# A two-layer decoder trunk in fp32: TensorE in the order of the program's text, and an order of the mixers made from stated latencies

## The chip, the core and the metric

The kernel runs on one core of a Trainium2 chip (trn2). Five engines work side by side, each through its own row of instructions: TensorE (PE, with its weight loads as PEld), VectorE (DVE), ScalarE (ACT), GpSimd (POOL) and SyncE (SP), which here only issues the DMAs that load weights. An engine starts its instructions in the order of its row, and a semaphore holds an instruction back until what it needs is done. The metric is device time in microseconds (us) of one execution, the median of several.

## What is computed

256 tokens of width 1024 go through two layers and a final norm. A layer is this (cut from the reference):

```python
def layer(x):                                   # x (1, 256, 1024), fp32
    x = x + 0.5 * swiglu_ffn(rms_norm(x), w_gate, w_up, w_down)     # ffn1, F = 2816
    h = rms_norm(x); z = h @ w_in               # one projection, columns split:
    y_a = mlstm_branch(...)                     # A: mLSTM matrix memory, 4 heads
    y_b = s5_branch(...)                        # B: S5 complex diagonal scan, then a GLU
    y_c = gla_branch(...)                       # C: gated linear attention, 4 heads
    y_d = rwkv7_branch(...)                     # D: RWKV-7 delta rule, 8 heads
    gates = sigmoid(gate_pre + gate_bias)       # 4 x 1024 columns of z
    merged = gates[0]*y_a + gates[1]*y_b + gates[2]*y_c + gates[3]*y_d
    x = x + merged @ w_out
    x = x + cross_attention(rms_norm(x), rms_norm(mem), wq, wk, wv, wo)  # 4 heads, 256 memory rows
    return x + 0.5 * swiglu_ffn(rms_norm(x), ...)                   # ffn2
```

All of it is in fp32. A product of fp32 accuracy is made of three products of rounded operands (`whi·xhi`, `whi·xlo`, `wlo·xhi`), so each block of weights costs three matmuls.

## The kernel before

**Tiling.** Activations stand transposed, as tiles of 128 channels by 256 tokens; `x` is eight of them. A matmul has a 128x128 block of weights and 256 columns. Weights come in chunks of 512 KB (`chunk`): SP loads one into one of three raw buffers `wraw`, ACT rounds it to `whi` (L243), DVE subtracts to get `wlo` (L244), both into one of four buffers, and TensorE multiplies. Half a megabyte of weights thus takes one ACT step and one DVE step and feeds 24 matmuls. A PSUM tile of 128x512 holds two products of 256 columns side by side.

**Stages of a layer.** `ffn1`: 22 products `gu` and the products `dn` back into `x` (L411). `mix`: the columns of `w_in` (`zin`), the four mixers and the gates. `mix_out`: four chunks of `wout` accumulated in four PSUM tiles `acc`; the last chunk adds each result to `x` (L579). `xattn`: queries `qps`, softmax, heads, and `wo` through the same `acc` code (`proj_k`). `ffn2` like `ffn1`. A norm needs the mean square of `x` for each token: eight squares (L292, L294), a matmul `ss` over the channels (L297), ten or eleven small DVE steps of a Newton iteration for the reciprocal root (L268 to L273), and a matmul `rp` that spreads the result over the partitions (L281).

**What sets the order.** Only SP's row is the order of the text (`manual_schedule` on SP alone). The rows of TensorE, DVE, ACT and POOL are made by a scheduler from dependencies, priorities and its own timeline; it may put a matmul of a later statement between two of an earlier one. In the mix the text itself is an interleaving: the mixers S (S5), G (GLA), M (mLSTM) and the dense work D (gates and the key and value products of the memory) are generators, and `ORDER` (L29 to L30) names for each layer which of them goes on next. RWKV (R) stands ahead of them all as one block. The four merges of the branches stand behind them.

**Places that the prediction steps through.** `gates` (L1522): for each of 16 chunks of a layer two products `gps` of 24 matmuls, side by side in one 128x512 tile, each followed by an ACT step `gst` (L1534). `proj_k` (L567): for `d` of 0 to 7 a product into half `d % 2` of tile `acc[d // 2]`, and in the last chunk the addition to `x` after each. In RWKV the small products with `thw` and `tha` (L1307 and on), the triangular solve `Tp` (L1417, L1419), the tiles `VU` and `Tw`. `mem_stats` (L444): the norm of the memory rows, called at `f == 10` of the first `ffn1`. `merge` (L1539): products `yps` and a DVE step `gld` (L1579).

Of the kernel before, what the change touches and what calls it, by code (L numbers as in the profile page):

```python
# [18 lines left out]
P = 128  # L19
# [6 lines left out]
MEM_AT = 0, 0  # L26
# [49 lines left out]
class K:  # L76
    def __init__(self, tc, ins, out, stages=None, layers=NL, taps=None):
        self.tc = tc
        self.nc = tc.nc
        self.ins = ins  # L80
        self.out = out
        self.layers = layers
        self.stages = stages
        self.taps = taps or {}
        self.uid = 0
        self.n_r, self.n_w, self.arena = 3, 4, 5248
        self.mem = self.kv = self.mcol = None
        self.loaded = False
        self.br, self.pdt = "n", ("psd", 2)
# [29 lines left out]
    def run(self):  # L119
        with ExitStack() as es:  # L120
# [12 lines left out]
            es.enter_context(self.tc.manual_schedule(engines={mybir.EngineType.SP}))  # L133
# [150 lines left out]
    def rstd_tok(self, x, last=False):  # L284

        nc = self.nc
        br, self.br = self.br, "n"
        ps = self.px([P, 512], "ss")
        acc = self.sp.tile([P, T], F32, tag="sa", name=self.nm("sa"), bufs=1)
        for k, xk in enumerate(self.tiles(x)):  # L290
            sq = acc if k == 0 else self.sp.tile([P, T], F32, tag="rA", name=self.nm("sq"), bufs=3)
            nc.scalar.activation(sq, xk, AF.Square)  # L292
            if 0 < k < (7 if last else 8):
                nc.gpsimd.tensor_tensor(acc, acc, sq, ALU.add)  # L294
        for tt in range(2):
            for i, s in enumerate((acc, sq) if last else (acc,)):
                nc.tensor.matmul(ps[:, 256 * tt:256 * tt + 1], s[:, tt * P:(tt + 1) * P], self.col[:, 0:1],  # L297
                                 start=(i == 0), stop=(i == int(last)))
# [6 lines left out]
    def rstd_row(self, x):  # L305

        rs = self.sp.tile([P, T], F32, tag="rs", name=self.nm("rs"), bufs=1)
        self.rows(self.rstd_tok(x), rs)
        return rs

# [18 lines left out]
    def norm(self, x, gname, rs=None):  # L329

        nc = self.nc
        rs = rs if rs is not None else self.rstd_row(x)
# [45 lines left out]
    def ffn(self, which):  # L378
# [6 lines left out]
        for f in range(22):  # L385
            blk = self.chunk(gu[l, f])
            ps = self.pd("gu")
            self.prod(blk, ps, hi, lo, f == 0)
            if f == 0:
                rs = self.rstd_row(self.x).unsqueeze(1).to_broadcast([P, 2, T])  # L390
# [7 lines left out]
            if f == 10 and self.mcol is None:  # L398
                self.mem_stats()
# [44 lines left out]
    def mem_stats(self):  # L444
# [3 lines left out]
        y = self.rstd_tok(self.mem_tiles())  # L448
        self.nc.vector.tensor_copy(self.mcol, y)
        self.rows(y, self.mrow)  # L450
# [7 lines left out]
    def mem_kv(self):  # L458
# [4 lines left out]
        for c in range(4):  # L463
            ps = self.pd("kps")
            self.prod(self.chunk(self.ins["wk"][l, c]), ps, mhi, mlo)
# [5 lines left out]
        for h in range(4):  # L471
            blk = self.chunk(self.ins["wv"][l, h])
            ps = self.pd("vps")
            for tt in range(2):
                for k in range(8):
# [13 lines left out]
    def xattn(self):  # L489
        nc, l = self.nc, self.l  # L490
        self.pdt = "psd", 2
        if self.kv is None:
            self.mem_gained()
            for _ in self.mem_kv():
                pass
# [11 lines left out]
        for c in range(2):  # L507
            q_of(c)
        y = self.rstd_tok(self.x)
# [3 lines left out]
        es = [self.softmax(0, qs, rq, kT)]  # L513
        q_of(2)
        es.append(self.softmax(1, qs, rq, kT))
        oh = [self.head(0, es[0], v)]
        q_of(3)
        for h in range(2, 4):
            es.append(self.softmax(h, qs, rq, kT))
            oh.append(self.head(h - 1, es[h - 1], v))  # L520
        self.proj_k("wo", 0, *oh[0], acc)
        oh.append(self.head(3, es[3], v))
        for h in range(1, 4):
            self.proj_k("wo", h, *oh[h], acc)
# [23 lines left out]
    def head(self, h, e, v):  # L548
# [7 lines left out]
        self.split(pt, *pT)  # L556
        ops = self.px([P, 2, T], "ops")
# [9 lines left out]
    def proj_k(self, wname, c, hi, lo, acc):  # L567
# [3 lines left out]
        for d in range(8):  # L571
# [31 lines left out]
    def wtiles(self, c):  # L603
        nc, l = self.nc, self.l
        self.mark(f"col{c}")
        blk = self.chunk(self.ins["win"][l, c])
        ps = self.pd("zin")
        if c < LAZY[self.l]:
            self.prod(blk, ps, *self.early, c == 0)
# [3 lines left out]
        self.prod(blk, ps, self.hi, self.lo)  # L613
        return ps

    def mix(self):
        nc, l = self.nc, self.l
        self.pdt = "psd", 2
        st = self.stages
        on = lambda s: st is None or "mix" in st or s in st  # L620
        self.early = self.gained(self.x, "mix_norm")
        with self.tc.high_priority():
            self.rs = self.rstd_row(self.x)
# [7 lines left out]
        with self.tc.issue_after(self.normed.ins):  # L631
            if on("mixd"):
                self.ys[3] = self.rwkv()
            live = {"S": on("mixb") and self.s5(), "G": on("mixc") and self.gla(), "M": on("mixa") and self.mlstm(),
                    "D": self.dense([b for b, n in ((2, "mixc"), (1, "mixb"), (0, "mixa"), (3, "mixd")) if on(n)])}
            branch = {"S": "s", "G": "g", "M": "g", "D": "d"}
            for c in ORDER[self.l]:
                if live[c]:
                    self.br = branch[c]
                    next(live[c], None)  # L640
            for c in "SGMD":
                self.br = branch[c]
                for _ in live[c] or ():
                    pass
        names = {2: "proj_c", 0: "proj_a", 1: "glu", 3: "proj_d"}
        for b in (2, 1, 0, 3):
            if b in self.ys:
                self.merge(b, self.ys[b], names[b])
# [4 lines left out]
    def dense(self, branches):  # L653

        for i, b in enumerate(branches):
# [1093 lines left out]
```

## Time and profile before

| | |
|---|---|
| runs | 1852.25, 1852.32, 1857.06 us; median 1852.32 |
| profiled execution | 1860.55 us, span of the profile 1858.8 us |
| busy over the span | PE 1794.1 us (97%), DVE 1302.3 (70%), ACT 912.2 (49%), POOL 527.5 (28%) |
| matmul instructions | 14884 in the trace |
| TensorE clock granted, mean | 0.979 |
| DMA | 320.35 MB, 172 GB/s mean |

A busy engine is not an engine at full rate: matmul records overlap, so the count of matmuls in a stretch says more than the busy time. The granted clock is the clock of TensorE as the profile records it; 1.00 is 2.4 GHz, and the lower of its two levels, 1.2 GHz, shows as 0.5 for the time that it lasts. The span lies 1.75 us under the execution's own time.

### The profile page before, as it was taken

How to read it: one execution, taken by the hardware profiler on the slowest of the kernel's cores; microseconds unless marked ns; L12 is line 12 of the kernel's file. 1: busy time of each engine (PE TensorE's matmuls, PEld its weight loads, DVE VectorE, ACT ScalarE, POOL GpSimd, SP SyncE). 2: the span in 40 equal slices, each digit the busy share in tenths (PEclk: the TensorE clock that was granted, in tenths of full speed). 3: DMA queues.
4: the chain of work that ended last, by engine and by line, in shares of the span. 5: the costliest groups of instructions: out<-in, count | busy, mean ns of one | idle time of the engine just before them, and what ended most of it. 6: DMA issues, size and time to landing. Idle time of an engine off the chain costs nothing.

```text
span 1858.8 us, 37108 instructions
## 1 busy us (share of the span) xinstructions
PE 1794.1 (97%) x14884; PEld 1757.8 (95%) x14884; DVE 1302.3 (70%) x2197; ACT 912.2 (49%) x1434; POOL 527.5 (28%) x733
## 2 busy tenths in 40 slices
PE   7989999989999999999999999999999999999997
PEld 7989998989999998999999999998989999999997
DVE  8876586896576776666597767696935667667653
ACT  4444455455554455444445445535544544545442
POOL 6699321150011210000154995103121103110001
PEclk9989999999999999999999999988989999999999
DMA  5656554537446654556556666644534676446653
GB/s 194 185 159 186 174 190 140 162 120 228 130 148 218 236 183 124 173 183 185 171 175 211 181 178 191 181 117 149 177 104 127 201 262 218 148 127 190 183 182 103
DMA packets 131853, 320.35 MB, mean 172 GB/s; under 512 B 45792, under 2 KB 50912, under 8 KB 131168
## 3 DMA queue, kind: packets, MB, share of 16 engines
q1 hardware_dynamic: 83664, 290.31, 50.2%
q10 hardware_dynamic: 48016, 27.67, 5.2%
q8 instruction: 116, 1.90, 0.4%
q14 instruction: 57, 0.47, 0.1%
HBM read 300.11 MB, written 16.52 MB: 170 GB/s over the span
## 4 chain that ended last, share of the span: by engine, by line
PE 51%; DVE 4%; issue 3%; DMA 2%; POOL 2%; ACT 1%; ACTq 0%; POOLq 0%; DVEq 0%
PE gu L259 6%; PE gu L258 6%; PE gu L260 6%; PE dn L258 3%; PE dn L259 3%; PE dn L260 3%; PE acc L576 2%; DVE wlo L244 1%; PE gps L259 1%; PE zin L258 1%; PE gps L258 1%; PE zin L260 1%; PE zin L259 1%; PE gps L260 1%; PE gu L354 1%
## 5 line engine op out<-in xcount | busy, mean ns | idle before, releaser
L244 DVE TENSOR_TENSOR wlo<-wraw,whi 128x1024 fp32r<-128x1024 f32 x524 | 673.7, 1287 | 352.3 <-ACT whi L243 345.3
L243 ACT CAST whi<-wraw 128x1024 fp32r<-128x1024 f32 x524 | 546.9, 1047 | 620.6 <-issue 154.7
L260 PE MATMUL gu<-xhi,wlo 128*128 128x256 f32 x1344 | 382.0, 284 | 2.9 <-DVE wlo L244 2.9
L258 PE MATMUL gu<-xhi,whi 128*128 128x256 f32 x1344 | 382.0, 284 | 0.0
L259 PE MATMUL gu<-xlo,whi 128*128 128x256 f32 x1344 | 381.7, 284 | 0.0
L260 PEld LDWEIGHTS gu<-xhi,wlo 128*128 128x128 f32 x1344 | 259.2, 193 | 3.5 <-DVE wlo L244 3.5
L258 PEld LDWEIGHTS gu<-xhi,whi 128*128 128x128 f32 x1344 | 259.1, 193 | 0.1
L259 PEld LDWEIGHTS gu<-xlo,whi 128*128 128x128 f32 x1344 | 259.1, 193 | 0.0
L294 POOL TENSOR_TENSOR arena<-arena 128x256 f32<-128x256 f32 x69 | 73.4, 1064 | 547.2 <-ACT arena L292 544.4
L260 PE MATMUL dn<-ahi,wlo 128*128 128x256 f32 x704 | 199.5, 284 | 1.0 <-DVE wlo L244 1.0
L258 PE MATMUL dn<-ahi,whi 128*128 128x256 f32 x704 | 199.2, 284 | 0.0
L259 PE MATMUL dn<-alo,whi 128*128 128x256 f32 x704 | 199.2, 283 | 0.0
L258 PE MATMUL gps<-hhi,whi 128*128 128x256 f32 x512 | 152.2, 298 | 4.5 <-ACT gst L1534 3.6
L259 PE MATMUL gps<-hlo,whi 128*128 128x256 f32 x512 | 150.2, 294 | 0.0
L260 PE MATMUL gps<-hhi,wlo 128*128 128x256 f32 x512 | 147.8, 290 | 0.0
L260 PEld LDWEIGHTS dn<-ahi,wlo 128*128 128x128 f32 x704 | 135.1, 192 | 1.4 <-DVE wlo L244 1.4
L259 PEld LDWEIGHTS dn<-alo,whi 128*128 128x128 f32 x704 | 135.1, 192 | 0.1
L258 PEld LDWEIGHTS dn<-ahi,whi 128*128 128x128 f32 x704 | 134.9, 192 | 0.3
L258 PE MATMUL zin<-hhi,whi 128*128 128x256 f32 x384 | 113.5, 296 | 4.1 <-ACT VU L1399 4.1
L260 PE MATMUL zin<-hhi,wlo 128*128 128x256 f32 x384 | 112.4, 293 | 0.0
L259 PE MATMUL zin<-hlo,whi 128*128 128x256 f32 x384 | 112.2, 292 | 0.0
L258 PEld LDWEIGHTS gps<-hhi,whi 128*128 128x128 f32 x512 | 101.0, 197 | 8.2 <-ACT gst L1534 5.0
(529 smaller groups left out, 4413.2 us busy)
## 6 DMA issues: line engine op xcount, KB each, us to landing
wraw<-in_gu_dram SPq DMA_DIRECT2D x176, 512.0 KB, 3.8
wraw<-in_dn_dram SPq DMA_DIRECT2D x88, 512.0 KB, 4.1
wraw<-in_win_dram SPq DMA_DIRECT2D x68, 512.0 KB, 4.1
wraw<-in_gates_dram SPq DMA_DIRECT2D x64, 512.0 KB, 4.1
gd<-gst ACTq DMA_DIRECT2D x32, 256.0 KB, 2.1
wraw<-in_wk_dram SPq DMA_DIRECT2D x16, 512.0 KB, 3.7
wraw<-in_wv_dram SPq DMA_DIRECT2D x16, 512.0 KB, 3.6
gld<-gd SPq DMA_DIRECT2D x32, 256.0 KB, 4.0
```

The costliest lines, as they stand in the source:

```text
L243: nc.scalar.copy(hi, raw)
L244: nc.vector.tensor_tensor(lo, raw, hi.bitcast(F32), ALU.subtract)
L258: nc.tensor.matmul(ps, w[0], x[0], start=first, stop=False)
L259: nc.tensor.matmul(ps, w[0], x[1], start=False, stop=False)
L260: nc.tensor.matmul(ps, w[1], x[0], start=False, stop=last)
L294: nc.gpsimd.tensor_tensor(acc, acc, sq, ALU.add)
L354: self.nc.tensor.matmul(ps[:, s, :], w[wi], x[xi], start=(k == 0 and s == 0 and i == 0), stop=(k == 7 and i == 2), skip_group_check=True)
L576: nc.tensor.matmul(ps, w[wi], x[:, k, :], start=(c == 0 and d % 2 == 0 and k == 0 and i == 0), stop=(c == 3 and k == 1 and i == 2), skip_g ...
```

## The change

TensorE joins SP in `manual_schedule`, so its row is the order of the text, and the text is written anew where that matters. In the mix, `ORDER` goes. `drive` goes through the generators R, S, G, M and, in the first layer, N (the memory's norm, moved here from `ffn1`). A generator yields a number: how long, in microseconds of TensorE work, the operands of its next piece will take. `pe_us` sums TensorE's work in the text so far at 0.12 us for a matmul of 256 columns, and `drive` takes the first generator whose time has come, else a piece of the dense work. `BEGIN` says when each generator starts. A yield of -1 asks for a turn at once, and after `SMALL` us of small work the dense work gets a turn.

```diff
-ORDER = ("SSDSSSDSSSGSDSSGSDSGDGDGDGDGDGDDGDGDGMDGMDGMMDMDMMDMDDDDDD",
-         "SSSSSSSSSSSSDSDGDGDGDMGDMGDMGDMGDMGDMGDMGDMGDGDGDDDDDDDDDD")
+BEGIN = {"R": 0, "S": 38, "G": 120, "M": 190, "N": 60}, {"R": 0, "S": 0, "G": 100, "M": 170, "N": 0}
+SMALL = 4.0
...
-            es.enter_context(self.tc.manual_schedule(engines={mybir.EngineType.SP}))
+            es.enter_context(self.tc.manual_schedule(engines={mybir.EngineType.SP, mybir.EngineType.PE}))
...
+    def drive(self):
+        t0 = self.pe_us()
+        gens = {"R": self.rwkv(), "S": self.s5(), "G": self.gla(), "M": self.mlstm()}
+        if self.mcol is None:
+            gens["N"] = self.mem_stats()
...
+        ready = {c: t0 + BEGIN[self.l][c] for c in gens}
+        dense, run = self.dense(gens), 0.0
+        while gens or dense:
+            t = self.pe_us()
+            can = [c for c in gens if ready[c] <= t]
+            if dense and (not can or run > SMALL and can[0] != "R"):
+                self.br, run = "d", 0.0
+                if next(dense, None) is None:
+                    dense = None
+                continue
+            c = can[0] if can else min(gens, key=ready.get)
+            self.br = branch[c]
+            lat = next(gens[c], None)
+            now = self.pe_us()
+            if lat is None:
+                del gens[c]
+            elif lat < 0:
+                ready[c], run = now, 0.0
+            else:
+                ready[c], run = now + lat, run + now - t
...
+    def pe_one(self, i):
...
+        return 0.12 * n / 256 if mov.dtype == F32R else 2 * 0.00084 * max(n, m, 32)
...
     def gates(self, br):
...
-            self.gated, self.gated2 = nc.scalar.dma_start(gd[dp], g), self.gated
-            yield
+                if s:
+                    self.gated, self.gated2 = nc.scalar.dma_start(gd[dp], g), self.gated
+                yield
...
-            if f == 10 and self.mcol is None:
-                self.mem_stats()
...
     def mem_stats(self):
...
+        sums = self.squares(self.mem_tiles())
+        yield 14
+        y = self.rstd_tok(sums)
         self.nc.vector.tensor_copy(self.mcol, y)
+        yield 6
         self.rows(y, self.mrow)
```

Besides: in an FFN the squares stand ahead of the products, `ss` stands behind product 1 and `rp` behind product 2, and the steps of the first three products on DVE and ACT are held back until then. In `xattn` the parts of the heads stand in another order. The merges of S and G move into the dense work, the gate columns 9, 10, 13 and 14 of `w_in` too, and all merges use the two PSUM buffers of the dense work where they had four of their own. In RWKV the tile `L` is split in two, with 16 DVE steps of half the size for each 8 and 4 more ACT DMAs in each layer, `VU` and `Kt` become separate tiles, the solve gets a high priority on DVE, and a yield of 45 stands ahead of the products with `Tw` that need it. The scratch arena shrinks from 5248 to 3776 columns. Both programs have the same 13946 matmul instructions.

What moved, at three places. First **TensorE in the gates** of layer 0, where a gate's chunk is multiplied; `gps` is the product's tile with its number, `hhi` and `hlo` the normed input. Before, the end of a half of tile 4734 and the start of the second half of tile 4660:

```order
L258 MATMUL gps_4734<-hhi_2775,whi 128x256
L259 MATMUL gps_4734<-hlo_2776,whi 128x256
L260 MATMUL gps_4734<-hhi_2775,wlo 128x256
L258 MATMUL gps_4660<-hhi_2775,whi 128x256 [waits Activation_49]
L259 MATMUL gps_4660<-hlo_2776,whi 128x256
L260 MATMUL gps_4660<-hhi_2775,wlo 128x256
```

Now, the end of the first half of tile 4927 and the start of its second half:

```order
L260 MATMUL gps_4927<-hhi_2842,whi 128x256
L261 MATMUL gps_4927<-hlo_2843,whi 128x256
L262 MATMUL gps_4927<-hhi_2842,wlo 128x256
L260 MATMUL gps_4927<-hhi_2842,whi 128x256 [waits Activation_49]
L261 MATMUL gps_4927<-hlo_2843,whi 128x256
L262 MATMUL gps_4927<-hhi_2842,wlo 128x256 [waits DVE_49]
```

Before, a half of another tile stood between the two halves of a tile; now the second half follows the first at once, and its first matmul waits for ACT, which reads the first half. This is so at 15 of the 32 chunks; at the others another branch's work stands between.

Second **TensorE at the end of `wout`** in layer 0, the last chunk, whose results DVE adds to `x`; `acc` with its number is the tile, `mghi` and `mglo` the merged input. Before, the even `d` of all four tiles (7305 to 7308) and then the odd ones; here the change from the one to the other:

```order
L576 MATMUL acc_7308<-mghi_7483,wlo 128x256
L576 MATMUL acc_7308<-mghi_7483,whi 128x256
L576 MATMUL acc_7308<-mglo_7484,whi 128x256
L576 MATMUL acc_7308<-mghi_7483,wlo 128x256
L576 MATMUL acc_7305<-mghi_7483,whi 128x256 [waits DVE_49]
L576 MATMUL acc_7305<-mglo_7484,whi 128x256
```

Now, tile 7328 with `d` = 0 and then `d` = 1:

```order
L624 MATMUL acc_7328<-mghi_7506,whi 128x256
L624 MATMUL acc_7328<-mglo_7507,whi 128x256
L624 MATMUL acc_7328<-mghi_7506,wlo 128x256
L624 MATMUL acc_7328<-mghi_7506,whi 128x256 [waits DVE_49]
L624 MATMUL acc_7328<-mglo_7507,whi 128x256
L624 MATMUL acc_7328<-mghi_7506,wlo 128x256
```

Before, 18 matmuls of three other tiles stood between the two halves of a tile; now the second half follows at once and waits for DVE's addition. The same holds for the other tiles and for `wo`: 16 places in two layers.

Third **the memory's norm**. TensorE before, in `ffn1`, where `ss` of the memory rows stands among the products `gu`:

```order
L259 MATMUL gu_1318<-xlo_138,whi 128x256
L260 MATMUL gu_1318<-xhi_137,wlo 128x256
L258 MATMUL gu_1318<-xhi_137,whi 128x256 [waits Activation_49]
L259 MATMUL gu_1318<-xlo_138,whi 128x256
L297 MATMUL ss_1081<-consts,arena 128x1 [waits PE_49,Pool_49]
L297 MATMUL ss_1081<-consts,arena 128x1
L260 MATMUL gu_1318<-xhi_137,wlo 128x256 [waits DVE_49]
L258 MATMUL gu_1318<-xhi_137,whi 128x256
```

TensorE now, in the mix of layer 0, at `rp` of the memory rows, 48 matmuls `gps` and 8 small ones behind `ss`:

```order
L260 MATMUL gps_3797<-hhi_2842,whi 128x256
L261 MATMUL gps_3797<-hlo_2843,whi 128x256
L262 MATMUL gps_3797<-hhi_2842,wlo 128x256
L283 MATMUL rp_3894<-consts,arena 128x128 [waits DVE_49,Activation_49]
L283 MATMUL rp_3894<-consts,arena 128x128
L1316 MATMUL yps_3898<-us_3440,s5In_1273 128x64 [waits PE_49]
L1316 MATMUL yps_3898<-us_3440,s5In_1273 128x64 x3
L260 MATMUL gps_3903<-hhi_2842,whi 128x256 [waits PE_49]
```

DVE before, in the same stretch of RWKV's work (`kk`, `KB`, `tha`) and S5's (`bb`, `ba`):

```order
L1239 SCALAR_TENSOR_TENSOR bb_4178<-consts,ba_4177 128x64 [waits DVE_49]
L1239 SCALAR_TENSOR_TENSOR bb_4178<-consts,ba_4177 128x64 x7
L244 TENSOR_TENSOR wlo<-wraw,whi 128x1024 [waits DMAHW2_49,PE_49,Activation_49]
L1351 SCALAR_TENSOR_TENSOR kk_3268<-tha_3237,kk_3268 128x1024 [waits DVE_49]
L1255 TENSOR_TENSOR arena<-arena,yps_4061 128x256 [waits DVE_49]
L1241 TENSOR_TENSOR ba_4177<-bb_4178,bC_469 128x512 [waits DVE_49]
L244 TENSOR_TENSOR wlo<-wraw,whi 128x1024 [waits DMAHW3_49,PE_49,Activation_49]
L1353 SCALAR_TENSOR_TENSOR KB_3310<-kk_3268,em_3266 128x8x64 [waits DMAHW4_49,DVE_49]
L1353 SCALAR_TENSOR_TENSOR KB_3310<-kk_3268,em_3266 128x8x64
L1355 TENSOR_SCALAR tha_3237<-tha_3237,arena 128x256 x4
L1242 TENSOR_TENSOR bb_4178<-bb_4178,bS_470 128x512 [waits DVE_49]
```

DVE now, from behind the step that reads `ss` of the memory rows:

```order
L1354 SCALAR_TENSOR_TENSOR bb_3848<-consts,ba_3847 128x64 [waits DVE_49]
L1354 SCALAR_TENSOR_TENSOR bb_3848<-consts,ba_3847 128x64 x5
L246 TENSOR_TENSOR wlo<-wraw,whi 128x1024 [waits DMAHW0_49,Activation_49]
L1354 SCALAR_TENSOR_TENSOR bb_3848<-consts,ba_3847 128x64 x2
L1469 SCALAR_TENSOR_TENSOR kk_3374<-tha_3194,kk_3374 128x1024 [waits DVE_49]
L270 TENSOR_SCALAR arena<-arena 128x2 [waits DVE_49]
L246 TENSOR_TENSOR wlo<-wraw,whi 128x1024 [waits DMAHW2_49,PE_49,Activation_49]
L1355 TENSOR_TENSOR ba_3847<-bb_3848,bC_469 128x512 [waits DVE_49]
L1368 TENSOR_SCALAR btz_3835<-btz_3835 128x256 [waits Activation_49]
L1471 SCALAR_TENSOR_TENSOR KB_3734<-kk_3374,em_3372 128x8x64 [waits DMAHW5_49,DMAHW7_49,DVE_49,Pool_49]
L1471 SCALAR_TENSOR_TENSOR KB_3734<-kk_3374,em_3372 128x8x64
L1473 TENSOR_SCALAR tha_3194<-tha_3194,arena 128x256 x4
```

The memory's `ss` and `rp` moved out of `ffn1` and into the stretch of the mix in which DVE's row holds RWKV's and S5's large steps, and the Newton steps (L270 and on) now stand between those.

## Rows read from the trace of the kernel before

**Rows 1.** The page: busy us and share of span; tenths in 40 slices.

```profile
PE 1794.1 (97%) x14884; PEld 1757.8 (95%) x14884; DVE 1302.3 (70%) x2197; ACT 912.2 (49%) x1434; POOL 527.5 (28%) x733
...
PE   7989999989999999999999999999999999999997
...
PEclk9989999999999999999999999988989999999999
```

**Rows 2.** Windows: stretch, length, busy us (instructions) per engine, clock, DMA.

```profile
100.00:120.00 20.00, 12.30 (x85) 12.31 (x86) 15.09 (x29) 9.72 (x17) 16.78 (x25) 0.74 0.52 150
226.00:660.00 434.00, 423.09 (x3604) 408.95 (x3603) 323.42 (x558) 222.91 (x361) 84.37 (x74) 0.99 0.56 175
...
660.00:700.00 40.00, 36.88 (x295) 35.35 (x294) 29.53 (x54) 22.00 (x37) 7.09 (x7) 1.00 0.58 184
...
800.00:820.00 20.00, 20.00 (x169) 20.00 (x168) 13.54 (x18) 9.52 (x14) 0.00 (x0) 1.00 0.58 184
...
1115.00:1570.00 455.00, 445.43 (x3684) 432.19 (x3683) 319.68 (x565) 227.65 (x368) 97.21 (x98) 0.96 0.55 171
1220.00:1240.00 20.00, 20.00 (x130) 19.66 (x130) 17.93 (x44) 8.80 (x13) 0.00 (x0) 0.74 0.28 81
```

**Rows 3.** TensorE's waits, whole span: us in total, times, longest.

```profile
PE ss L297 <- POOL arena L294: 8.7, 1, 8.7
...
PE zin L258 <- ACT VU L1399: 4.1, 1, 4.1
...
PE gps L258 <- ACT gst L1534: 3.6, 3, 2.7
...
PE rp L281 <- DVE arena L273: 2.4, 1, 2.4
PE px L1440 <- DMA Tw<-dW: 2.4, 1, 2.4
PE yps L1248 <- DVE ba L1244: 2.1, 1, 2.1
...
PE px L770 <- POOL gQ L760: 1.4, 1, 1.4
```

**Rows 4.** ScalarE by line and shape: count, busy us, mean ns, idle before.

```profile
L243 ACT CAST whi<-wraw 128x1024 fp32r<-128x1024 f32 x524 | 546.9, 1047 | 620.6 <-issue 154.7 <-PE dn L259 78.1 <-PE gu L259 58.1
...
L1534 ACT ACTIVATE gst<-gps,arena 128x256 f32<-128x256 f32 x64 | 30.0, 472 | 3.6 <-PE gps L260 3.4
```

**Rows 5.** VectorE by line and shape, columns as in the group above.

```profile
L244 DVE TENSOR_TENSOR wlo<-wraw,whi 128x1024 fp32r<-128x1024 f32 x524 | 673.7, 1287 | 352.3 <-ACT whi L243 345.3 <-DMA s5In<-s5G 2.4 <-DMA ud<-bup 2.2
...
L326 DVE SCALAR_TENSOR_TENSOR xlo<-x,consts,xhi 128x256 fp32r<-128x256 f32 x64 | 42.6, 684 | 10.2 <-ACT xhi L325 10.0
...
L579 DVE TENSOR_TENSOR x<-acc,x 128x256 f32<-128x256 f32 x32 | 12.9, 418 | 4.1 <-PE acc L576 4.0
L1579 DVE SCALAR_TENSOR_TENSOR gld<-gld,yps 128x512 f32<-128x512 f32 x16 | 10.8, 683 | 6.2 <-PE yps L260 6.0
```

**Rows 6.** VectorE's timeline in the mix of layer 0: start us, us.

```profile
330.23 1.56 DVE L1239 TENSOR_TENSOR_SCAN bb<-consts,ba 128x64 f32<-128x64 f32 x8
...
332.82 1.22 DVE L1351 SCALAR_TENSOR_TENSOR kk<-tha,kk 128x1024 f32<-128x1024 f32 x1
...
336.03 1.29 DVE L1353 SCALAR_TENSOR_TENSOR KB<-kk,em 128x512 f32<-128x512 f32 x2
337.23 3.25 DVE L1355 TENSOR_SCALAR tha<-tha,arena 128x256 f32<-128x256 f32 x4
```

**Rows 7.** VectorE's timeline in the first FFN, first and late Newton step.

```profile
29.07 0.15 DVE L300 TENSOR_SCALAR arena<-ss 128x2 f32<-128x2 f32 x1
...
38.23 0.18 DVE L273 SCALAR_TENSOR_TENSOR arena<-arena 128x2 f32<-128x2 f32 x1
```

**Rows 8.** TensorE's timeline just after the wait for `mem_stats`.

```profile
109.36 0.41 PE L260 MATMUL gu<-xhi,wlo 128*128 128x256 f32 x1
...
109.57 0.41 PE L258 MATMUL gu<-xhi,whi 128*128 128x256 f32 x1
```

More of the change, by code (lines that the diff above doesn't have):

```diff
@@ L631, in mix @@
         with self.tc.issue_after(self.normed.ins):
[L632 to L645, printed above, removed]
+            self.drive()
         for b in (2, 1, 0, 3):
-            if b in self.ys:
-                self.merge(b, self.ys[b], names[b])
+            for _ in self.merge(b):
+                pass
         self.x = self.hp.tile([P, 8, T], F32, name=self.nm("x"))
@@ new lines, in dense @@
+    def dense(self, gens):
+        self.open = {}
+        for i, b in enumerate((2, 1, 0, 3)):
+            for j, _ in enumerate(self.gates(b)):
+                yield 1
+            for c in {1: (9, 10), 0: (13, 14)}.get(b, ()):
+                ps = self.wtiles(c)
+                th = self.open[c] = self.ot([P, 2, T], n="th")
+                self.nc.scalar.activation(th, ps, AF.Tanh, scale=0.5)
+                if b == 1:
+                    self.nc.vector.scalar_tensor_tensor(th, th, 1.0, ps, ALU.add, ALU.mult)
+                yield 1
+        if "S" not in gens:
+            yield from self.merge(1)
+        self.now = self.gated
+        with self.tc.issue_after(self.now.ins):
+            self.mem_gained()
+        if "G" not in gens:
+            yield from self.merge(2)
+        for _ in self.mem_kv():
+            yield 1
@@ L886, in mlstm @@
             for hp in range(2):
+                yield 2.5 if i or hp else 12
                 ps = self.px([P, 2, T])
@@ L945, in mlstm @@
                                         base=0, channel_multiplier=-1)
+        yield 1
+        decays(0)
+        for h in range(4):
+            yield 3 if h else 4
             sc = self.px([P, 512])
@@ L1245, in s5_tile, with s5_out @@
         V(ss[:, 1, :], a[:, 1, :], b[:, 0, :], ALU.add)
-        for j in range(4):
-            for ri in range(2):
-                nc.tensor.matmul(yps[:, j, 1:64], Cp[:, j, ri].rearrange("p a b -> p (a b)"),
-                                 ss[:, ri, 64 * j:64 * j + 63], start=False, stop=(ri == 1), skip_group_check=True)
-        yield
-        th = sp.tile([P, T], F32, tag="bth", bufs=1)
+        return ss
+    def s5_out(self, i, yps, y):
+        nc = self.nc
+        tz = self.ot([P, 2, T], n="btz", bufs=2)
+        th, z = tz[:, 0], tz[:, 1].rearrange("p (j k) -> p j k", k=64)
         tv = th.rearrange("p (j k) -> p j k", k=64)
@@ L1507, in rwkv @@
         for jp in range(2):
+            yield 4 if jp else 22
             tp_ = self.px([P, 2, T])
```

355 lines of the change are left out of this document (214 added, 141 removed).

## Prediction

> **What bounds the kernel now.** I read the page first. TensorE is busy 97% of the span, VectorE 70%, the rest less [rows 1]: TensorE is the bound, and a change of order can only give back, or add, time in which TensorE stands still or runs at its lower clock. How much is there to give back? A window deep in an FFN shows the full rate: 169 matmuls of 256 columns in 20 us, 0.118 us each, at clock 1.00, although VectorE is busy only 13.5 of the 20 [rows 2]. Where TensorE has its operands, nothing else matters. So the whole question is where it does not have them.
>
> The windows by stage answer this. The mix of layer 0 leaves TensorE idle for 434 − 423.1 = 10.9 us, that of layer 1 for 455 − 445.4 = 9.6 us [rows 2]. The mean clock there is 0.99 and 0.96. As a mean of the levels 1 and 0.5, 0.96 says that 8% of 455 us, 36 us, ran at 1.2 GHz. One window shows what that means: 130 matmuls in 20 us at 0.74 [rows 2], and single matmuls start 0.21 us apart [rows 8]. So 36 us at the lower level lose 36 × (1 − 0.118/0.21) = 16 us, and layer 0 loses 4 us in the same way. Together the mixes hold 20 us of idle time and 20 us of clock. The list of TensorE's waits names the rest: 8.7 us for the squares of `mem_stats` in `ffn1`, and in the mixes 4.1 for `VU`, 3.6 for `gst`, 2.4 for `Tw`, 2.1 for `ba`, 1.4 for `gQ` and smaller ones [rows 3].
>
> **What the change takes away.** (a) The memory's norm leaves `ffn1`. The window that holds its wait has 85 matmuls where 169 fit [rows 2]: 84 × 0.118 = 9.9 us, and 1 us of the wait lies ahead of the window: **−11**. (b) The yields let other work stand between a mixer's step and the matmul that needs it. If they are well chosen, the waits for `VU`, `Tw`, `ba`, `gQ` and their like go; I take 15 of the 20 us of idle time (the rest is `gst` and weights), between 0 and −15, likeliest **−15**, since the offsets and yields ask for more distance than the steps take. The lower clock came after such waits, so part of it goes too: between 0 and −20, taken **−10**, the middle.
>
> **What it adds.** TensorE now takes the order of the text literally, and at several places the text puts a matmul directly behind the one whose result another engine must read first. Before, the scheduler had put other matmuls between. Behind a waiting matmul stand all later ones, the dense ones too; the weight loads run on until the four buffers are full, so nothing is later there but TensorE.
>
> (c) Gates, 15 places. The second half of a tile waits for `gst` on the first half. `gst` takes 0.47 us [rows 4]; that is the least. If a cast of weights stands ahead of it on ScalarE, 1.05 us more [rows 4]: 1.5. I take 1.0, as casts stand in that row often (524 of them against 64 `gst`): 15, from 7 to 23. The 3.6 us that TensorE waited for `gst` before [rows 3] go off: **+11**. That such a wait is real, though the halves are different columns of a tile, the same row shows: three times `gps` waited for `gst`.
> The Trainium skill, "PSUM — Partial Sum Buffer", section "PSUM bank collisions raise a hardware error", says that a different address in the same bank and quadrant still collides, so an engine's read of one half and TensorE's write of the other must be kept apart. The order of the changed kernel shows such a wait at each place, and the three waits agree; by that rule the term stands, and without it the sum below would be less by (c), (d) and (e).
>
> (d) `wout` and `wo`, 16 places. Each odd `d` waits for the addition to `x` of the even one. The addition takes 0.42 us [rows 5]; with one step `xlo` of the next norm ahead on VectorE 1.1, with a `wlo` ahead too 2.4 [rows 5]. At 1.1 each it is 17.6 us, from 6.7 to 38. But VectorE has these steps to do anyway before the next stage can start, and the old order waited for them just behind: TensorE idles 3.1 us in the window at the end of the first `wout` [rows 2], taken as 12 for the four such stretches. Net **+5**, from −5 to +26.
>
> (e) RWKV's small products with `thw` and `tha`: 8 places with the same short return, an ACT step of the size of `gst` ahead, only the other of the pair between. 0.6 each, **+5**, from 4 to 12.
>
> (f) The memory's norm in the mix. Between the memory's `ss` and its `rp` stand 48 products, 5.7 us, and 8 small ones, some 7 us in all. VectorE has in its row between them, by the order: eight scans 1.56, three `wlo` of 1.23 to 1.29, `kk` 1.22, a pair `KB` 1.29, four `tha` 3.25 [rows 5, 6], together 11; a second pair `KB` 1.3; twelve steps that take no less than 0.42 each, 5; and the Newton steps, which alone with their hops take 2.4 [rows 3]. 20 us against 7: a wait of **13** for `rp`, and 2 more for the lower clock that followed the like wait in `ffn1` (109.36 and 109.57 [rows 8]): **+15**. It is 6 if VectorE has done half of these steps by then, and 20 if it comes late to them.
>
> (g) The same cover of 48 products (5.7 us) now stands between `ss` and `rp` in every FFN. In the first, where S5's preparation shares VectorE, the Newton steps took from 29.07 to 38.41, 9.3 us [rows 7]: +3.6. In the others VectorE has less beside; 0 to 3.6 each, 0.5 taken: **+5**, from 4 to 14.
>
> (h) The last merges. With two PSUM buffers a product `yps` waits for the `gld` of the one before the last, and the `wlo` of the next weights stand behind `gld` steps on VectorE. At three of eight products in a layer the row holds one or two such steps more, 0.68 each [rows 5], and a `wlo`: 0.7 to 2 us, six times, taken as **+6**, from 0 to 12.
>
> Edits at nothing: the eight more DMAs and the halved `L` steps cost VectorE perhaps 3 us in the mix, hidden under the yield of 45 us that the text gives the solve; if that cover is gone, the products with `Tw` wait by that much. The held-back steps of the first three FFN products land on an otherwise half idle VectorE.
>
> **The sum.** −11 − 15 − 10 + 11 + 5 + 5 + 15 + 5 + 6 = **+11 us**. The profiled execution, 1860.55 us, would become 1871.5; it lies 8 above the median of the runs, so on the median's scale 1852.3 + 11 = **1863**.
>
> **The rivals.**
> Faster: in the mix VectorE is the second bound, and short waits of TensorE at (c) to (e) only let VectorE get ahead, so that later waits for `wlo` shrink by as much. Then (c) to (e) come to +4 in all, (f) to +8, (h) to 0, and (b) brings 28: −11 − 28 + 4 + 8 + 5 = −22, 1830. For it: layer 1's mix loses 26 us now [rows 2], and VectorE is at 70% over all [rows 1]. Against it: the places in (c) stand mostly in dense stretches, where a half before and after has all its weights, so that there is nothing to get ahead of. If the second half of a tile had not to wait at all, (c) to (e) would go: 11 − 21 = −10, 1842; the three waits for `gst` [rows 3] speak against it.
>
> Same: the short waits cost half of what I take, (c) to (e) +10, the rest as in the sum: 0, 1852.
>
> Much slower: the short waits come in rows (four in 9 us at `wout`, three gate chunks running), and each row lowers the clock as the longer waits did. If another 36 us run at 1.2 GHz, as in the mix of layer 1 now, and (b) brings no clock back: +11 + 16 + 10 = +37, 1889. It decides from the point where a granted clock under 1 shows in the stretches of `acc` and `gps` that are at 1.00 now (660 to 700 [rows 2]).
>
> That the plan does not hold is a rival within these: the yields count TensorE at full rate, and a stretch that runs slower only gives the operands more time, so an order that misses does so where VectorE's row is long, as in (f).
>
> **How the numbers follow.** About 0.3% (5.6 us) is what a measurement of this kernel can tell from no change. Forecast, between 6 and 25 us slower: 0.38. Much slower: 0.16. Same: 0.15. Faster: 0.31, of which the halves free of each other are 0.03. So slower 0.54, same 0.15, faster 0.31. The range runs from 1822, 8 us under the faster rival, which is itself no sharper than that, to 1895, a little above the much slower one; about 0.1 stays outside on either side. The forecast's own range, between its neighbours, is 1858 to 1878.
>
> **What would show it.** In the trace of the changed kernel: no wait for the memory's squares near 100 us, and 160 or more matmuls in that window (a); `gps` waiting for `gst` at 15 places with 0.5 to 1.5 us (c); `acc` waiting for `x` at 16 places (d); one wait of 6 to 20 us for the Newton steps in the mix of layer 0 (f); a longer wait for `rp` in `ffn1` (g). It is wrong if the list of waits shows under 15 us for `gst` and `x` together, if `rp` in the mix does not wait, or if the granted clock in the mixes rises to 0.99 in both: then the faster rival holds. It is wrong on the other side if the clock falls where it is 1.00 now.

## The result

The changed kernel takes 1929.74 us (median; 1925.74 to 1931.87), the kernel before 1853.05 us in the same comparison: a ratio of 1.041, 95% interval 1.039 to 1.043. It is slower, as forecast, but by 77 us and not by 11, and outside the range. The profiled execution took 1928.87 us, its span is 1926.8, 68.0 more than before.

The page of the changed kernel, busy time and tenths in 40 slices, beside [rows 1]:

```profile
PE 1794.6 (93%) x14884; PEld 1756.7 (91%) x14884; DVE 1296.7 (67%) x2205; ACT 918.3 (48%) x1442; POOL 539.8 (28%) x741
...
PE   6999988797999989999999999989999988989997
...
PEclk9999999898999999999999999999999999999999
```

TensorE is busy for the same 1794 us; it only stands still longer. The tenths of PE show where: slices 6 to 10 (240 to 480 us), the mix of layer 0, above all. Over the whole span the granted clock is not the cause: its mean is 0.975, it was 0.979. In the mix of layer 0 it did fall, and the other stages gave that time back; the windows of this one stage, before and after, are:

```profile
230.70:650.30 419.60, 408.79 (x3486) 394.86 (x3485) 312.56 (x549) 217.19 (x354) 82.76 (x73) 0.99 0.56 175
```

```profile
220.20:692.20 472.00, 421.54 (x3494) 407.04 (x3494) 311.85 (x565) 222.82 (x367) 87.02 (x84) 0.95 0.50 157
```

So of the 52 us that the stage is longer, 13 are longer busy time and 40 are standing still.

The stages, by the start of each on TensorE's timeline (us):

| stage | before | after | change |
|---|---|---|---|
| start and `ffn1` of layer 0 | 230.7 | 220.2 | −10.5 |
| mix of layer 0 | 419.6 | 472.0 | +52.4 |
| `wout` and `xattn` of layer 0 | 86.6 | 96.5 | +9.9 |
| `ffn2` and the next `ffn1` | 396.1 | 392.7 | −3.4 |
| mix of layer 1 | 429.4 | 446.0 | +16.6 |
| `wout` and `xattn` of layer 1 | 87.4 | 96.4 | +9.0 |
| `ffn2` of layer 1 and the end | 209.0 | 203.0 | −6.0 |

The kernel before has its first `gu` ahead of the last 20 matmuls of `wo`, so that some 2 us of +9.9 and −3.4, and of +9.0 and −6.0, are a shifted border.

TensorE's waits in the changed kernel (us in total, times, longest), against [rows 3]:

```profile
PE gps L260 <- ACT gst L1663: 37.8, 17, 4.7
PE rp L283 <- DVE arena L275: 16.7, 5, 10.0
PE acc L624 <- DVE x L627: 14.9, 16, 1.5
PE px L1088 <- POOL anum L1075: 8.0, 4, 6.3
PE gu L375 <- ACT whi L245: 8.0, 1, 8.0
PE yps L262 <- DVE wlo L246: 7.0, 5, 2.1
PE px L1419 <- ACT thw L1421: 6.4, 4, 2.1
...
PE yps L1316 <- DVE btz L1371: 3.5, 2, 2.3
PE px L912 <- POOL go L896: 3.5, 2, 2.4
```

All the waits of this view add up to 125 us; the same view of the kernel before adds up to 57. The difference, 68 us, is the 68 us of the span. So the whole loss is in this list, and nearly all of it in places where the text puts a matmul too close behind what it needs. What was to go did go: `VU`, `Tw`, `gQ` and the memory's squares are not in the list, and the window that held that last wait is full, 169 matmuls where there were 85 [rows 2]:

```profile
100.00:120.00 20.00, 20.00 (x169) 20.00 (x168) 14.82 (x18) 9.51 (x14) 20.00 (x32) 1.00 0.66 198
```

### The profile page after: what moved, and what is told of

It reads as the page before. It is cut to its first block, busy times and chain, and to the rows that moved or that the text cites. A ratio compares the mean times of both kernels' runs of the same rounds, so it can differ in the third digit from the quotient of the medians.

```text
span 1926.8 us, 37160 instructions
## 1 busy us (share of the span) xinstructions
PE 1794.6 (93%) x14884; PEld 1756.7 (91%) x14884; DVE 1296.7 (67%) x2205; ACT 918.3 (48%) x1442; POOL 539.8 (28%) x741
## 5 line engine op out<-in xcount | busy, mean ns | idle before, releaser
L261 PE MATMUL gu<-xlo,whi 128*128 128x256 f32 x1344 | 380.8, 283 | 0.0
L261 PEld LDWEIGHTS gu<-xlo,whi 128*128 128x128 f32 x1344 | 258.6, 192 | 0.0
L294 POOL TENSOR_TENSOR arena<-arena 128x256 f32<-128x256 f32 x69 | 69.3, 1004 | 571.3 <-ACT arena L292 569.4
L261 PE MATMUL dn<-alo,whi 128*128 128x256 f32 x704 | 199.2, 283 | 0.0
L260 PE MATMUL gps<-hhi,whi 128*128 128x256 f32 x512 | 157.5, 308 | 37.8 <-ACT gst L1663 37.8
L261 PE MATMUL gps<-hlo,whi 128*128 128x256 f32 x512 | 151.8, 296 | 0.0
L260 PEld LDWEIGHTS gps<-hhi,whi 128*128 128x128 f32 x512 | 105.2, 205 | 43.0 <-ACT gst L1663 41.3
L261 PEld LDWEIGHTS dn<-alo,whi 128*128 128x128 f32 x704 | 135.1, 192 | 0.0
L261 PE MATMUL zin<-hlo,whi 128*128 128x256 f32 x384 | 109.3, 285 | 0.0
```

What stands on the lines that cost most here:

```text
L260: nc.tensor.matmul(ps, w[0], x[0], start=first, stop=False)
L261: nc.tensor.matmul(ps, w[0], x[1], start=False, stop=False)
```

## The experiments

The theory behind the prediction: each matmul that the text puts right behind the reading of its tile costs a return to another engine, and such waits add up. The rivals: the mix is short of VectorE, so that a wait taken away comes back elsewhere; or it is not the order but the rest of the change that costs. Times are medians; the ratio is to the kernel before on the same chip (the changed kernel: 1.041).

**Two tiles for the halves of a gate chunk.** The largest wait, and nothing else.

```diff
-            ps = self.pd("gps")
             g = self.ot([P, 2, T], n="gst", bufs=3)
             for s in range(2):
+                ps = self.pd("gps")
```

> The changed kernel, but each half of a gate chunk goes into a PSUM tile of its own, so that 24 matmuls of the other half stand between a half and the next use of its tile. Theory A (the order of the text makes TensorE wait for gst, and nothing else is short there): the 37.8 us of waits for gst fall under 6, the clock of layer 0's mix rises from 0.95, and the time falls by 32 to 45, to about 1890. Theory B (VectorE and ScalarE are the bound of the mix, a wait at gst only moves): gst falls, but waits for wlo or whi grow by as much, and the time falls by less than 12.

1893.36 us, ratio 1.0235 (1.020 to 1.027): 36 us less by the medians, 32 by the ratios. No wait for `gst` is left; the first rows of the list are now:

```profile
PE rp L283 <- DVE arena L275: 19.0, 4, 12.0
PE acc L624 <- DVE x L627: 15.5, 16, 1.5
PE px L1419 <- ACT thw L1421: 9.6, 4, 3.6
```

The longest wait for `rp` is 12.0 here and was 10.0, and `thw` grew from 6.4 to 9.6. The whole list falls from 125 to 97 us: 38 went with `gst`, 10 came back in other waits. The other 8 of the 36 us are busy time of TensorE (1786.2 us for 1794.6, at a mean clock of 0.978 for 0.975). Theory A. The Trainium skill, "PSUM — Partial Sum Buffer", section "PSUM bank collisions raise a hardware error", has the rule behind the wait (a different address in the same bank and quadrant still collides). This run agrees in so far as the same products with the halves in different tiles wait no more; no run here lets the two meet, so the collision itself is not shown.

**Why was a wait for `gst` 2.2 us, when I had taken 1.0?** ScalarE's timeline of the changed kernel at one of the waits, and the matmul that waited:

```profile
454.58 1.04 ACT L245 CAST whi<-wraw 128x1024 fp32r<-128x1024 f32 x1 [1.45 <-PE gps L261]
...
455.53 0.47 ACT L1663 ACTIVATE gst<-gps,arena 128x256 f32<-128x256 f32 x1
```

```profile
456.05 0.38 PE L260 MATMUL gps<-hhi,whi 128*128 128x256 f32 x1 [1.39 <-ACT gst L1663]
```

The cast `whi` of later weights stands ahead of `gst` in ScalarE's row. It is itself waiting for TensorE (`<-PE gps L261`): its buffer comes free with the last matmuls of the very half that `gst` reads. So at each such place the return is cast plus `gst`, 1.05 + 0.47, and the wait 1.39. First I tried to move `gst` ahead by priority:

```diff
-                nc.scalar.activation(g[:, s, :], ps[:, s, :], AF.Tanh, bias=self.gb[:, br * 8 + d:br * 8 + d + 1],
-                                     scale=0.5)
+                with self.tc.high_priority():
+                    nc.scalar.activation(g[:, s, :], ps[:, s, :], AF.Tanh, bias=self.gb[:, br * 8 + d:br * 8 + d + 1],
+                                         scale=0.5)
```

> The changed kernel, the order of TensorE untouched, but gst gets a high priority in ScalarE's row. Theory A1 (a wait for gst is long because casts whi and RWKV's steps stand ahead of it in ScalarE's row): the 17 waits of 2.2 us shrink to 0.6 to 0.9 each, 10 to 15 in all, and the time falls by 20 to 30. Theory A2 (the return from TensorE to ScalarE and back is itself that long): they stay above 1.5 each, and the time falls by less than 10.

1924.14 us, ratio 1.040 (1.036 to 1.044), 34.5 us of waits for `gst`: neither theory's number, because the edit did not do its work. The casts have the same high priority, and in the trace they still stand ahead at 16 of the 17 waits. So the order was written out:

```diff
-                    nc.scalar.copy(hi, raw)
+                    g = self.gst_at.get(self.w_at - 1 - self.n_w)
+                    if g is not None:
+                        with self.tc.issue_after(g):
+                            nc.scalar.copy(hi, raw)
+                    else:
+                        nc.scalar.copy(hi, raw)
...
-                nc.scalar.activation(g[:, s, :], ps[:, s, :], AF.Tanh, bias=self.gb[:, br * 8 + d:br * 8 + d + 1],
-                                     scale=0.5)
+                self.gst_at[self.w_at - 1] = nc.scalar.activation(
+                    g[:, s, :], ps[:, s, :], AF.Tanh, bias=self.gb[:, br * 8 + d:br * 8 + d + 1], scale=0.5).ins
```

> The changed kernel with ScalarE's row alone altered: each cast whi that would take the weight buffer of a half of a gate chunk stands behind gst of that half, not ahead of it. Theory A1 (a wait for gst is the cast plus gst, 1.05 + 0.47, because the cast stands ahead in ScalarE's row and its buffer comes free at the same matmul): the waits at which a cast stood ahead fall from 1.4 to 0.4 each, all of them from 37.8 to some 20, and the time falls by 14 to 22. Theory A2 (the return itself is that long): they stay, and the time moves by less than 5.

1909.11 us, ratio 1.029 (1.027 to 1.031): 21 us less, with TensorE's order untouched. The same place:

```profile
453.52 0.47 ACT L1669 ACTIVATE gst<-gps,arena 128x256 f32<-128x256 f32 x1 [1.55 <-PE gps L268]
453.89 1.04 ACT L249 CAST whi<-wraw 128x1024 fp32r<-128x1024 f32 x1
```

```profile
454.04 0.39 PE L266 MATMUL gps<-hhi,whi 128*128 128x256 f32 x1 [0.56 <-ACT gst L1669]
```

The wait is 0.56 now, `gst` and 0.1 us of way; all of them fell from 37.8 at 17 places to 24.0 at 13. That is theory A1, and it agrees with the Trainium skill, "Perfetto Trace Analysis", section "Tensor Engine Instruction (MATMUL, LD_WEIGHTS)", which calls ScalarE's row strictly first in, first out. What is left are mostly the long waits (eight of 0.9 to 4.3 us), and their rows in the changed kernel show what else stands ahead:

```profile
318.28 0.42 ACT L292 ACTIVATE arena<-mraw 128x256 f32<-128x256 f32 x1 [5.39 <-DMA mraw<-in_memT_dram]
...
318.91 1.03 ACT L245 CAST whi<-wraw 128x1024 fp32r<-128x1024 f32 x1
319.85 0.47 ACT L1663 ACTIVATE gst<-gps,arena 128x256 f32<-128x256 f32 x1
...
441.42 1.28 ACT L1663 ACT_TABLE_LOAD   x1
442.72 0.47 ACT L1663 ACTIVATE gst<-gps,arena 128x256 f32<-128x256 f32 x1
443.09 0.39 ACT L827 ACTIVATE gA<-consts,arena 128x128 f32<-128x128 f32 x1
...
444.26 1.26 ACT L827 ACTIVATE gA<-consts,arena 128x128 f32<-128x128 f32 x4
445.42 1.03 ACT L245 CAST whi<-wraw 128x1024 fp32r<-128x1024 f32 x1
446.36 0.47 ACT L1663 ACTIVATE gst<-gps,arena 128x256 f32<-128x256 f32 x1
```

```profile
446.88 0.58 PE L260 MATMUL gps<-hhi,whi 128*128 128x256 f32 x1 [4.71 <-ACT gst L1663]
```

At 318 the squares of the memory rows, which the change has moved here, wait 5.4 us for their load, with the cast and `gst` behind them and TensorE behind `gst` (4.2 us). The longest wait, 4.7 us, ends at 446.88: ahead of the `gst` that it needs stand the end of a table load, the `gst` of the chunk before, eight steps `gA` of GLA and a cast. These long ones were read, not isolated by a run.

**Even and odd `d` at the end of `wout` and `wo`.**

```diff
-        for d in range(*ds):
+        for d in sorted(range(*ds), key=lambda d: d % 2) if c == 3 else range(*ds):
```

> The changed kernel, but the last chunk of wout and wo takes the even d and then the odd, as the scheduler had it before. Theory A: the 14.9 us of waits for x go and the time falls by 12 to 16. Theory B (VectorE has the additions and xlo to do in any case, my offset of 12 us): the waits move to the first products behind (qps, gu), and the time falls by 0 to 5.

1933.67 us, ratio 1.045 (1.042 to 1.049): no gain. The 16 waits for `x` are gone, and two rows have come that the list of the changed kernel does not have:

```profile
PE qps L375 <- DVE xlo L348: 7.8, 4, 2.7
PE gu L375 <- DVE xlo L348: 7.1, 4, 2.6
```

7.8 + 7.1 = 14.9, as much as `x` before it; that it agrees to the tenth is chance. Here theory B holds: VectorE has the additions and `xlo` of the next norm to do before the next stage can run, and in the text's order TensorE waits for them on one side of the stage's border or on the other. The list as a whole is 4 us shorter than that of the changed kernel; the time is not, because TensorE is busy for 1801.6 us where it was for 1794.6, at a mean clock of 0.969 where it was 0.975. The old order lost less there: its list has 4.0 us for `xlo` in these two rows. Its rows show the scheduler mixing the first products of the next stage into the last of `wo`:

```profile
736.88 0.28 PE L354 MATMUL gu<-xhi,whi 128*128 128x256 f32 x1
737.00 0.28 PE L576 MATMUL acc<-ohi,whi 128*128 128x256 f32 x1
```

That this mixing is what saves the time fits the rows; no run has it alone.

**The memory's `rp` later.**

```diff
-        yield 6
+        yield 40
         self.rows(y, self.mrow)
```

> The changed kernel, but the memory's rp gets a yield of 40 instead of 6, so that it stands some 550 matmuls behind ss instead of 48. Theory A: the 10.0 us wait for the Newton steps goes, and some lower clock behind it: the time falls by 10 to 16. Theory B: VectorE's row is the bound there, other products wait in its place, and the time falls by less than 5.

1916.37 us, ratio 1.036 (1.032 to 1.040): 9 us less by the ratios, 13 by the medians. The wait of 10 is gone; the four smaller ones for `rp`, in the FFNs and the final norm, are left:

```profile
PE gps L260 <- ACT gst L1663: 41.6, 18, 5.0
...
PE rp L283 <- DVE arena L275: 7.2, 4, 3.1
```

`gst` took 4 back. Mostly theory A. Why `rp` waited stands in VectorE's timeline of the changed kernel, row by row what the order had shown:

```profile
347.75 0.41 DVE L1371 SCALAR_TENSOR_TENSOR btz<-btz,yps 128x256 f32<-128x256 f32 x1
348.09 1.28 DVE L1476 TENSOR_TENSOR KB<-k,em 128x512 f32<-128x512 f32 x2
349.29 0.15 DVE L274 SCALAR_TENSOR_TENSOR arena<-arena 128x2 f32<-128x2 f32 x1
349.36 1.66 DVE L1501 SCALAR_TENSOR_TENSOR r<-r,consts,k 128x256 f32<-128x256 f32 x4
350.95 0.15 DVE L275 SCALAR_TENSOR_TENSOR arena<-arena 128x2 f32<-128x2 f32 x1
```

Newton steps of 0.15 us between groups of steps of RWKV and S5 that take 1.3 to 1.7.

**Both together.** The edits of the first run and of the one just above.

> Two tiles for the halves of a gate chunk and the memory's rp with a yield of 40, together. Theory A (each wait of the order returns itself, they add up): 36 and 13 us under the changed kernel, about 1881. Rival (both feed on the same slack of VectorE in the mix of layer 0): 1888 or more.

1910.79 us, ratio 1.029 (1.027 to 1.032): worse than the two tiles alone. The number is the rival's, but it was not reached by its mechanism alone. The trace has a wait of a length that no other run has, in `ffn1`, which neither edit touches:

```profile
PE wps L1265 <- ACT s5W L1266: 13.9, 2, 13.2
```

```profile
188.37 0.58 ACT L1266 COPY s5W<-wps 128x512 f32<-128x512 f32 x1 [12.70 <-POOL s5Bp L1237]
```

With the two tiles alone the same copy waits 0.24 us:

```profile
175.24 0.59 ACT L1266 COPY s5W<-wps 128x512 f32<-128x512 f32 x1 [0.24 <-PE wps L1265]
```

A copy for S5's preparation waits 12.7 us for GpSimd's long row, TensorE behind it. The rows of ScalarE and GpSimd have the same steps in the same order up to there in both runs, as far as the traces name them; why the copy waits for a later step of GpSimd in this kernel stays open. With 13 off it would be near the run of the two tiles: so of the gain of the later `rp` nothing is seen here. The waits for `rp` fell by 12 (19.0 to 7.1), but three others on VectorE rose by as much: `yps` for `btz` from 1.3 to 7.0, `dn` for `wlo` from nothing to 4.3, `px` for `rows` from 1.6 to 3.9. That much is the rival's. A further run below returns to this.

**All the yields.** The edits above, and:

```diff
                 nc.tensor.matmul(pa[:, s, :], up[64:128, j * P:(j + 1) * P], wg[64:128, 0, :], start=True, stop=True)
+            for s in range(2):
+                j = 2 * jp + s
                 nc.scalar.activation(thw[:, j, :], pw[:, s, :], AF.Tanh, bias=hv[:, j:j + 1], scale=0.5)
...
-            yield 2 if hp else 12
+            yield 2 if hp else 20
             while 9 + hp not in self.open:
...
-            yield 2 if hp else 10
+            yield 2 if hp else 24
             while 13 + hp not in self.open:
...
-            if f == 2:
+            if f == 3:
                 rs = self.row(y).unsqueeze(1).to_broadcast([P, 2, T])
-            if f >= 2:
+            if f >= 3:
```

> As the run with tiles and memory, and: thw and tha have all four products ahead of the four ScalarE steps; the yields ahead of the transposes of go and anum are 20 and 24 instead of 12 and 10; in the FFNs rp stands behind product 3 instead of 2. Theory A: the waits for thw (6 to 9 us), anum and go (11), rp in the FFNs (4) go, and the time falls by 15 to 22 against that run, to about 1862, still not under the kernel before, because the waits for x in wout and wo (15) and for wlo in the last merges (7) stay. Rival (the engines behind are the bound): less than 8.

1866.66 us, ratio 1.007 (1.004 to 1.010): 44 us less, 13 of them the long wait of the run before, which this kernel does not have. The other 31 are more than theory A's 15 to 22; that the time still lies near its 1862 is luck, since 1862 is 19 under the 1881 that was expected for the run before. Of the 38 us by which the span fell, 27 are waits and 11 busy time, at a mean clock of 0.983 where it was 0.977. The waits for `thw`, `anum` and `go` are gone and `rp` is down to 3.8. Of what the change had added there stays mainly

```profile
PE acc L624 <- DVE x L627: 15.6, 16, 1.5
...
PE yps L262 <- DVE wlo L246: 7.7, 4, 2.1
PE px L1460 <- DVE rows L1454: 6.1, 1, 6.1
```

and the last of these is not in the list of the changed kernel. Six small edits of the order take back 63 of the 77 us.

**The same without the later `rp`.**

> Run e6 without the memory's later rp (its yield is 6 again), all else as there. Theory A (the wait for rp is worth itself and the clock behind it, as in the run that altered it alone, 13 us): 1876 to 1882. Rival (in an order with few other waits left VectorE's row is shorter at that place, or the later rp collides with something else, as in the run of tiles and memory): 1862 to 1870.

1870.02 us, ratio 1.009 (1.006 to 1.011), against 1.007 (1.004 to 1.010): 3 us, within the measurement. Yet `rp` waits again:

```profile
PE rp L283 <- DVE arena L275: 11.9, 2, 9.5
```

So the wait of 9.5 is worth some 3 here, where it was worth 9 to 13 in the changed kernel. This is nearer to the rival. The two lists add up to the same, 82.4 us here and 82.6 with the later `rp`: the 8 us that it takes off `rp` come back there in small waits, the largest 3.6 (`yps`) and 2.6 (`dn` for `whi`). The 3 us are TensorE's busy time (1779.7 and 1776.6 us). Why those small waits come stays open.

**TensorE free again.** The new text, but the scheduler makes TensorE's row (one buffer for `gst`, for want of memory).

```diff
-engines={mybir.EngineType.SP, mybir.EngineType.PE}
+engines={mybir.EngineType.SP}
...
-            g = self.ot([P, 2, T], n="gst", bufs=3)
+            g = self.ot([P, 2, T], n="gst", bufs=1)
```

> The changed text, but TensorE's row is again made by the scheduler (SP alone in the order of the text; gst has one buffer, since its memory is short). Theory A (the order of the text as such costs, at the places where the text puts a matmul right behind the one whose result is read): gst, x, thw and rp waits nearly go, and the time is within 15 of the kernel before. Rival (the new text, fewer buffers and the moved parts cost): it stays above 1890.

1860.44 us, ratio 1.0036 (1.002 to 1.005). One engine less in that list undoes 69 of the 77 us: with the scheduler's order the parts that were moved, split and given smaller buffers cost some 7 us together, and the rest goes with the order of the text. The list now starts with

```profile
PE gps L260 <- ACT gst L1663: 9.9, 9, 2.7
PE yps L262 <- DVE wlo L246: 9.5, 5, 2.1
```

and `x`, `thw`, `anum` and `go` are not among its longer rows. With two tiles for the gates besides:

> TensorE's row made by the scheduler from the new text, and two tiles for the halves of a gate chunk. Theory A: the 9.9 us that TensorE still waits for gst there go, and the time falls from 1860 to 1848 to 1854, no slower than the kernel before. Rival (VectorE's share in the mix is the bound there): 1858 or more.

1854.56 us, ratio 1.002 (0.9998 to 1.0035), no longer to be told from the kernel before. The waits for `gst` are gone from the list, and the time lies at the edge of theory A's range. The fall itself is 6 us by the medians and 4 by the ratios, whose intervals overlap, so that theory A is likelier here and not shown.

**Term (a) in the kernel before.** One line: the memory's norm at `f == 18` in place of `f == 10`.

> The kernel before, with one line altered: the memory's norm is called at product 18 of the first FFN instead of 10, when GpSimd is through with S5's preparation. Theory A (the 8.7 us wait for its squares was worth 11 us, my term a): the time falls by 8 to 12, to about 1842. Rival (GpSimd's row keeps the squares late wherever they are called, or another wait takes the place): less than 4.

1852.41 us, ratio 1.000 (0.999 to 1.001). The rival: the wait is still there, at 162 us where it was at 108,

```profile
PE ss L297 <- POOL arena L294: 8.8, 1, 8.8
```

since GpSimd's row keeps the squares late among the steps of S5's preparation, which run on to 189 us. Together with two tiles for the gates:

> As the run before with the memory's norm at product 18, and two tiles for the halves of a gate chunk. Theory A: the 3.6 us of waits for gst go too, another 2 to 6 us, about 1838. Rival: the scheduler has filled these places already, no difference above 2.

1857.26 us, ratio 1.003 (1.001 to 1.005): 5 us more, which neither theory had. There the wait for the squares is not among the longer rows, but TensorE waits 13.1 us for `wlo` in the FFN in its stead. None of the runs beats the kernel before.

## Why the prediction was wrong in size

The direction and the places were right: the list of waits after has the places of (c) to (h). The counts were right for (d) and (f); (e) has 4 waits and not 8. For (c) the 17 near my 15 are luck: in the trace the second half stands right behind the first at 11 of the 32 chunks, not at 15, and waits at all 11 (29.9 us); the other six waits (7.9 us) have another branch's products ahead of them, where I had counted none. The sizes, term by term, us:

| term | forecast | measured |
|---|---|---|
| (a) memory's norm out of `ffn1` | −11 | stage −10.5, with (g) in it |
| (b) waits of the mixers | −15 | `VU`, `Tw`, `ba`, `gQ` and two more gone, −15; but see below |
| (b) clock of the mixes | −10 | layer 0 from 0.99 to 0.95, busy time +12.7; layer 1 from 0.96 to 0.97, −6.4; together +6 |
| (c) gates, before the 3.6 are taken off | 15 at 15 places | 37.8 at 17 |
| (d) `wout`, `wo` | 17.6, net +5 | 14.9; stages +9.9 − 3.4 + 9.0 − 6.0 = +9.5 |
| (e) `thw`, `tha` | +5 at 8 places | 6.4 at 4 |
| (f) `rp` of the memory | 13 of wait | 10.0 |
| (g) `rp` in the FFNs | +5 | 16.7 − 10.0 − 2.4 at the end as before = 4.3 |
| (h) last merges | +6 | `yps` for `wlo`, `whi`, `gld`: 7.0 + 1.9 + 0.9 |
| not in the sum | 0 | `anum` and `go` 11.5, `btz` 3.5 |

The largest differences are 23 us in (c), 15 in waits that were not in the sum and 16 in the clock of (b). Four steps failed. **First, (c)**: I priced a wait at 1.0 us between the end with `gst` alone and the end with one cast ahead, 1.5, because casts stand in that row "often". The row of ScalarE could be read in the order as well as TensorE's, and in the trace it has a cast ahead of `gst` at all 17 places. At eight of them nothing else stands ahead, and the wait is 0.3 to 1.4 us, 7.8 in all: these lie within my ends or under them. At the other nine more steps stand ahead of the cast, and the wait is 1.8 to 4.7 us, 30.0 in all. The upper end was not an end: 2.2 on average. Two runs bear on it: without the shared tile 36 us go, with `gst` ahead of the cast 21.

**Second, what was left out**: the transposes of `anum` and `go` wait for GpSimd behind a Newton chain, 11.5 us. The text gives them yields of 10 and 12; I had looked at the yields as covers that are generous ("ask for more distance than the steps take"), and that sentence was wrong: for `anum` and `go` they ask for less. Greater yields in the run with all of them took these two waits away. The 3.5 us for `btz` were left out too.

**Third, (b)'s clock**: I took half of the clock's loss as gained with no row for it. In layer 0, where the waits came, the mean clock of 226 to 660 fell to 0.95. By the stage it cost 12.7 us of busy time there, and layer 1 gave back 6.4, so that the term is +6 and not −10. The window has 3245 matmuls where there were 3604 [rows 2], the most of it from standing still (388.06 us busy where it was 423.09):

```profile
226.00:660.00 434.00, 388.06 (x3245) 374.35 (x3244) 293.33 (x545) 210.84 (x352) 75.02 (x76) 0.95 0.50 154
```

**Fourth, the range.** The upper ends of the terms add up to some 90 us over the kernel before, and the measured 77 is inside. I drew the range from the rivals' likeliest times instead, and so cut off a side on which every single term had room.

Of the rivals, the faster one fell: short waits of TensorE did not let VectorE get ahead in a way that later pays, since when the gates' 37.8 us of waits went, only 10 came back in other waits and the time fell by 36. It did hold in one place, at the border of `wout` and `xattn`, where the run with even and odd `d` gave nothing. The much slower one gave 1889 with a mechanism, the clock, that did not act over all (0.975 against 0.979). Its sign, a clock under 1 in 660 to 700, is there by the letter (0.91), but these 40 us now hold the end of the mix: the stage with `acc` reads 1.00 in layer 0, as before, and 1.00 in layer 1, where it was 0.98. Its time was nearest, but the time was lost in waiting.

## What to carry to other kernels

An order written by hand replaces every small thing that a scheduler did, also those that nobody had asked for: here it had kept the halves of a tile apart. Before pinning an engine, look for each pair of neighbours on it of which the second waits for a reader of the first, and price the return by the whole row of the reading engine, with what stands ahead there, not by the reading step. A yield is a forecast of such a return, and a list of waits by pair tells after one run which yields are too short. If the upper ends of independent terms all point one way, the range has to reach toward their sum.

## What the runs showed of the hardware

The bare return from TensorE to ScalarE and back costs little more than the reading step: a wait of 0.56 us for a `gst` of 0.47. With a cast of 1.05 us ahead of it in ScalarE's row the wait was 1.39. And a place that an edit leaves alone can still change: in the run of tiles and memory one copy in ScalarE's row, far from both edits and behind the same steps as before, waited 12.7 us for GpSimd and cost TensorE 13.2 us; why is not shown.
